# Two of the four weight-quarter sums of each up-projection pair made by accumulating transfers

## The chip, the core and the metric

The kernel runs on one core of one Trainium2 chip. The metric is the device time of one execution in microseconds (us); the runs of the kernel before took 2460.62, 2461.86 and 2464.46 us, so the median is 2461.86 us. Engines are named as in the profile: PE does the matmuls and PEld loads their weights, DVE is the vector engine, ACT the scalar engine, POOL the general one. SP does no arithmetic here and only issues transfers; POOL issues transfers too, from a queue of its own. Every engine works through its own instructions strictly in order, and waits on semaphores of the others.

## The reference, cut to what matters

One layer of a decoder with a model width of 2048, for 512 prompt positions and 8 x 8 sampled ones (576 columns in all). The change touches one product only, `rmsnorm(x, g_ffn) @ w_up`:

```
x  = x + concat(a_out, b_out) @ w_out
up = rmsnorm(x, g_ffn) @ w_up                    # 2048 -> 2 * 5632 = 11264
upc = causal_dwconv(concat(ffn_hist, up), w_dw_f) + b_dw_f    # width 3
x  = x + (silu(upc[..., :5632]) * upc[..., 5632:]) @ w_down
gate = sigmoid(rmsnorm(x, g_ple) @ w_ple_gate)
x  = x + gate * (p @ w_ple_proj)
```

## The kernel before, in words

All tensors are 32-bit floats. The weights stream from memory once, in units of 512 KB: eight tiles of 128x128, side by side, land in one of five buffers of a ring (`raw`), by a transfer that SP issues (`load_unit`, L189). Half a unit (four tiles, 128x512) is a piece. Each piece is split in two by `prepare`: ACT copies it, rounded, to `wh` (L244), and DVE subtracts that from the source to get `wl` (L245); there are four buffers of each. Each weight tile then meets three matmuls: `wh` with the high part of the activations, `wh` with their low part, `wl` with the high part (in the up stage L710, L711 and L712). `weights` calls `prepare` three pieces ahead of the tile in use, and `prepare` calls `add_up` up to two pieces further ahead. These calls set program order; a scheduler then sets each engine's order, and the engines run ahead of one another as far as buffers allow.

The stages, one after another: `mix` (w_in), `out` and `out2` (w_out), `proj` (w_ple_proj), `up` (w_up), four `down` stages, `ple` and a tail. The up stage is 44 pairs. A pair makes the 128 gate channels and the 128 value channels of one hidden tile from 16 x 2 weight tiles, by a scheme with seven products where a plain one has eight: the 16 row tiles are taken as even and odd ones, the two halves of the 576 columns are combined beforehand (`sum_in`, tiles `sx`), and the weights of a pair fall into four quarters of 512 KB, one unit each. Written as a0, a1 (gate channels, even and odd rows) and b0, b1 (value channels), the seven products, in their order, use

- product 5: b0 + b1, in a tile of its own, `sum`
- product 7: b0 + a0, written over b0 in its raw buffer
- product 6: b0 + b1 + a0, written over `sum`
- product 1: a0 as it is
- product 3: b0 + b1 + a1, written over `sum`
- product 4: b1 as it is
- product 2: a1 as it is

A product is 8 weight tiles (2 pieces) x 3 matmuls of 288 columns, so a pair has 14 pieces and 168 matmuls. The four sums are eight DVE additions of 128x512 a pair, all issued at L218: `sum<-raw,raw` for product 5, `raw<-raw,raw` for product 7, `sum<-sum,raw` for products 6 and 3.

The two `sum` tiles of a pair lie in spare places (`SPARE`): two activation tiles `xh`/`xl` for every second pair, and the places of `res14` and `res15` for the others, the first pair among them. Those two are read last by ACT at L580 (`xg`, a step of `sum_in`), shortly before the up stage.

Results of the products are combined at L723 to L733: ACT copies product 1 (`ua`), DVE makes the rest. Product 3's and product 4's results share one PSUM tile, and L729 reads product 3's. The results of 22 of the pairs go to memory by two POOL transfers each (`upd`, L735 and L736); those of the other 22 go through a convolution and a gate, and then to memory by one POOL transfer (`hidd`, L739). In the last pair, 12 hidden tiles are fetched back (`hq`) and split by ACT and DVE (`hh` at L677, `hl` at L678) for the down stages. Around the start of the up stage, 16 POOL transfers (`pjd`, L898) write the results of `proj` from `pa`, which ACT copies out of PSUM (L897), and 16 SP transfers (`xs`) read the new x back for the norm.

Of the kernel before, what the change touches and what calls it, by code (L numbers as in the profile page):

```python
# [11 lines left out]
ALU = mybir.AluOpType  # L12
PSUM = bass.MemoryType.PSUM

P = 128
# [11 lines left out]
NF = DFF // P  # L27
# [33 lines left out]
SUB = 4  # L61


def plan():

    groups = []

    def add(phase, w, outs, ks):  # L70
        groups.append((phase, [(w, m) for m in outs], list(ks)))

    ks = range(KT)

    def gate(i):
        return NA + i

    def val(i):
        return i

    def vee(j):
        return 3 * NA + j

    def you(j):
        return 2 * NA + j

    add("mix", "w_in", [gate(0), val(0), gate(1)], ks)
    add("mix", "w_in", [val(1)], ks)
    for i in range(2, NA):
        add("mix", "w_in", [vee(i - 2)], ks)  # L90
        add("mix", "w_in", [you(i - 2)], ks)
        add("mix", "w_in", [gate(i)], ks)
        add("mix", "w_in", [val(i)], ks)
    add("mix", "w_in", [vee(NB - 2)], ks)
    add("mix", "w_in", [you(NB - 2)], ks)
    add("mix", "w_in", [vee(NB - 1), you(NB - 1)], ks)

    early = [k for k in range(KT) if k not in LATE]
    add("out", "w_out", [0, 1, 2], early)
    for m in range(3, KT):  # L100
        add("out", "w_out", [m], early)
    add("out2", "w_out", [0, 1, 2], LATE)
    for m in range(3, KT):
        add("out2", "w_out", [m], LATE)

    for m in range(KT):
        add("proj", "w_ple_proj", [m], range(DPLE // P))
    for j in range(NF):
        add("up", "w_up", [j, NF + j], ks)

    at = 0
    for c, n in enumerate(CHUNKS):
        js = ORDER[at : at + n]
        at += n
        add(f"down{c}", "w_down", [0, 1, 2], js)
        for m in range(3, KT):
            add(f"down{c}", "w_down", [m], js)

    add("ple", "w_ple_gate", [0, 1, 2], ks)
    for m in range(3, KT):  # L120
        if m not in LAST:
            add("ple", "w_ple_gate", [m], ks)
    for m in LAST:
        add("tail", "w_ple_gate", [m], ks)
    return groups


def weight_order():

    tiles, pieces = [], []
    for phase, outs, ks in plan():
        n = len(tiles)
        if phase == "up":
            (w, a), (_, b) = outs
            for m, odd in ((b, 0), (b, 1), (a, 0), (a, 1)):
                tiles += [(w, k, m) for k in range(odd, KT, 2)]
            pieces += [(n // UNIT, prod, half) for prod in PRODS for half in range(2)]
        else:  # L140
            tiles += [(w, k, m) for k in ks for w, m in outs]
            for s in range(-(-n // SUB), -(-len(tiles) // SUB)):
                pieces.append((s * SUB // UNIT, s % 2))
    assert len(tiles) % UNIT == 0
    return tiles, pieces
# [3 lines left out]
def trunk_kernel(ctx: ExitStack, tc: tile.TileContext, A, O):  # L149
    nc = tc.nc  # L150
    groups = plan()
    order, pieces = weight_order()
    n_w = len(order)

# [4 lines left out]
    def tl(shape, tag, name, bufs=1, dt=F32):  # L159
        return pool.tile(shape, dt, tag=tag, name=name, bufs=bufs)  # L160

    def tmp(name, shape=(P, 2, HT)):
        return tl(list(shape), "t", name, bufs=6)


    raws, parts = {}, {}
# [7 lines left out]
    SPARE = [f"xh{LATE[2]}", f"xl{LATE[2]}", f"res{KT - 2}", f"res{KT - 1}"]  # L174
# [6 lines left out]
    def load_unit(u):  # L181
        if u in raws or u * UNIT >= n_w:
            return
        t = tl([P, UNIT * P], "raw", f"raw{u}", bufs=5)
        if u == 0:
            nc.sync.dma_start(t[:, : SUB * P], A["wstream"][u][:, : SUB * P])
            nc.sync.dma_start(t[:, SUB * P :], A["wstream"][u][:, SUB * P :])
        else:
            nc.sync.dma_start(t, A["wstream"][u])  # L189
        raws[u] = t  # L190

    sums = {}


    NEEDS = {5: 1, 7: 2, 6: 2, 1: 2, 3: 3, 4: 3, 2: 3}

    def quarter(u, n, half):
        return raws[u + n][:, half * SUB * P : (half + 1) * SUB * P]

    def add_up(s):  # L200

        if s in summed_w or s >= len(pieces) or len(pieces[s]) == 2:
            return
        u, prod, half = pieces[s]
        for a in range(NEEDS[prod] + 2):
            load_unit(u + a)
        if prod in (1, 2, 4):
            return
        if prod == 7:
            out = a = quarter(u, 0, half)  # L210
            b = quarter(u, 2, half)
        elif prod == 5:
            out = sums[half] = tl([P, SUB * P], SPARE[2 * (u // 4 % 2) + half], f"sum{u}_{half}")
            a, b = quarter(u, 0, half), quarter(u, 1, half)
        else:
            out = a = sums[half]
            b = quarter(u, 2 if prod == 6 else 3, half)
        nc.vector.tensor_tensor(out=out, in0=a, in1=b, op=ALU.add)  # L218
        summed_w[s] = out

    summed_w = {}

    def prepare(s):
        if s in parts or s >= len(pieces):
            return
        for a in range(s, s + 3):
            add_up(a)
        p = pieces[s]
        if len(p) == 2:
            for a in range(4):  # L230
                load_unit(p[0] + a)
            src = raws[p[0]][:, p[1] * SUB * P : (p[1] + 1) * SUB * P]
        elif s in summed_w:
            src = summed_w[s]
        else:
            src = quarter(p[0], {1: 2, 2: 3, 4: 1}[p[1]], p[2])
        spare = s - (len(pieces) - 4)
        if spare < 0:
            h = tl([P, SUB * P], "wh", f"wh{s}", bufs=4, dt=F32R)
            l = tl([P, SUB * P], "wl", f"wl{s}", bufs=4, dt=F32R)  # L240
        else:
            h = tl([P, SUB * P], HID[32 + 2 * spare], f"wh{s}", dt=F32R)
            l = tl([P, SUB * P], HID[33 + 2 * spare], f"wl{s}", dt=F32R)
        nc.scalar.activation(h, src, AF.Copy)  # L244
        nc.vector.tensor_tensor(out=l, in0=src, in1=h.bitcast(F32), op=ALU.subtract)  # L245
        parts[s] = (h, l)
# [3 lines left out]
    def weights(i=None):  # L250

        n = at["tile"] if i is None else at["tile"] + i
        s = n // SUB
        for a in range(s, s + (4 if s >= 3 else 2)):
            prepare(a)
        if i is None:
            at["tile"] += 1
        h, l = parts[s]
        o = n % SUB * P
        return h[:, o : o + P], l[:, o : o + P]  # L260
# [502 lines left out]
    for gi, (phase, outs, ks) in enumerate(groups):  # L763
# [66 lines left out]
        if gi == 0:  # L830
            prepare(0)
            split_in(0, x0[0], v("g_mix", 0))
            split_in(1, x0[1], v("g_mix", 1))
# [36 lines left out]
        for n, (w, m) in enumerate(outs):  # L870
# [24 lines left out]
            elif w == "w_ple_proj":  # L895
                a = tmp(f"pa{m}")
# [159 lines left out]
```

## Time and profile before

| what | value |
|---|---|
| runs | 2460.62, 2461.86, 2464.46 us |
| profiled execution: time, span | 2461.64 us, 2459.9 us |
| PE busy | 2429.7 us (99%), 18200 matmuls |
| DVE busy | 1838.9 us (75%) |
| ACT busy | 1099.0 us (45%) |
| POOL busy | 92.7 us (4%) |
| traffic | 294.70 MB, mean 120 GB/s |
| up stage | 679.4 to 1677.7 us of the span |

The span is the time between the first and the last event of the profiled execution; 1.7 us of that execution's time lie outside of it. Busy shares are averages over stages with different limits. In rows of the profile a group of instructions is given as line, engine, operation, output and inputs, shapes and count, then busy time, mean time of one, and the idle time before them with what ended it. Rows of a window list give the busy time and count of each engine in a stretch, then the clock that PE was granted (1.00 is full), the share of the 16 transfer engines that was busy, and GB/s.

### The profile page before, as it was taken

The page shows a single profiled execution, that of the slowest core. Times are in us where ns is not written, and L with a number is a line of the kernel's source. Part 1 is how long each engine was busy: PE and PEld are TensorE (multiplying, and loading weights), DVE is VectorE, ACT ScalarE, POOL GpSimd, SP SyncE. Part 2 cuts the span into 40 slices and gives each one's busy share as a digit, 9 for nine tenths or more (in the row PEclk, how much of TensorE's full clock was granted, in tenths as well). Part 3 has the DMA queues.
Part 4 walks back from the last instruction along what each step waited for, and adds up shares of the span by engine and source line. Part 5 has one row for each costly group of instructions (what it writes and reads, how often), then busy time and mean ns, then how long its engine had stood idle before and what let it go on. Part 6 is the DMA issues. An engine that isn't in the chain of part 4 may idle for free. (4 is left out here: it accounts for less than half of the span.)

```text
span 2459.9 us, 45459 instructions
## 1 busy us (share of the span) xinstructions
PE 2429.7 (99%) x18200; PEld 2413.7 (98%) x18200; DVE 1838.9 (75%) x3243; ACT 1099.0 (45%) x2028; POOL 92.7 (4%) x175
## 2 busy tenths in 40 slices
PE   9999999999999999999999999999999999999997
PEld 8999999999999999999999999999999999999997
DVE  7877788885898888888988888887559762254545
ACT  6444445433764454444544444454335441243334
POOL 1000000000200000000000000000000000000000
PEclk9999999999999999999999999999999999999999
DMA  6332222332653334333333333347434442222332
GB/s 237 95 84 84 83 84 84 127 114 89 219 197 119 110 103 126 116 109 117 106 128 114 103 124 111 110 165 269 120 99 150 127 126 86 81 83 86 112 100 96
DMA packets 106196, 294.70 MB, mean 120 GB/s; under 512 B 23568, under 2 KB 27792, under 8 KB 105984
## 3 DMA queue, kind: packets, MB, share of 16 engines
q1 hardware_dynamic: 96096, 259.20, 33.6%
q0 software_dynamic: 9744, 32.60, 3.7%
q8 instruction: 142, 2.33, 0.4%
q14 instruction: 70, 0.57, 0.1%
q10 hardware_dynamic: 144, 0.01, 0.0%
HBM read 255.43 MB, written 36.32 MB: 119 GB/s over the span
## 5 line engine op out<-in xcount | busy, mean ns | idle before, releaser
L244 ACT ACTIVATE wh<-raw 128x512 fp32r<-128x512 f32 x792 | 500.7, 633 | 974.5 <-PE acc L850 669.8
L245 DVE TENSOR_TENSOR wl<-raw,wh 128x512 fp32r<-128x512 f32 x792 | 541.7, 686 | 302.6 <-ACT wh L244 300.9
L710 PE MATMUL acc_up<-sx,wh 128*128 128x288 f32 x2464 | 733.2, 298 | 3.1 <-ACT wh L244 1.5
L712 PE MATMUL acc_up<-sx,wl 128*128 128x288 f32 x2464 | 724.4, 296 | 4.9 <-DVE wl L245 4.8
L711 PE MATMUL acc_up<-sx,wh 128*128 128x288 f32 x2464 | 727.6, 295 | 0.0
L710 PEld LDWEIGHTS acc_up<-sx,wh 128*128 128x128 f32 x2464 | 464.6, 189 | 9.7 <-DVE ua L729 2.6
L712 PEld LDWEIGHTS acc_up<-sx,wl 128*128 128x128 f32 x2464 | 463.4, 189 | 6.4 <-DVE wl L245 6.3
L711 PEld LDWEIGHTS acc_up<-sx,wh 128*128 128x128 f32 x2464 | 464.5, 189 | 0.1
L848 PE MATMUL acc<-xh,wh 128*128 128x288 f32 x1984 | 427.3, 296 | 5.4 <-ACT wh L244 5.3
L850 PE MATMUL acc<-xl,wh 128*128 128x288 f32 x1984 | 424.0, 295 | 0.3 <-DVE xl L286 0.3
L852 PE MATMUL acc<-xh,wl 128*128 128x288 f32 x1984 | 423.5, 294 | 0.0
L848 PEld LDWEIGHTS acc<-xh,wh 128*128 128x128 f32 x1984 | 318.0, 188 | 7.6 <-ACT wh L244 5.3
L850 PEld LDWEIGHTS acc<-xl,wh 128*128 128x128 f32 x1984 | 319.1, 188 | 0.8 <-DVE xl L286 0.6
L852 PEld LDWEIGHTS acc<-xh,wl 128*128 128x128 f32 x1984 | 318.1, 188 | 0.3 <-issue 0.3
L852 PE MATMUL acc<-hh,wl 128*128 128x288 f32 x1408 | 300.9, 295 | 0.0
L848 PE MATMUL acc<-hh,wh 128*128 128x288 f32 x1408 | 300.5, 295 | 0.4 <-DVE x1r L891 0.4
L850 PE MATMUL acc<-hl,wh 128*128 128x288 f32 x1408 | 300.7, 295 | 0.0
L244 ACT ACTIVATE wh<-sum 128x512 fp32r<-128x512 f32 x264 | 166.5, 631 | 224.7 <-PE acc_up L711 212.7
L245 DVE TENSOR_TENSOR wl<-sum,wh 128x512 fp32r<-128x512 f32 x264 | 181.7, 689 | 100.9 <-ACT wh L244 100.8
L848 PEld LDWEIGHTS acc<-hh,wh 128*128 128x128 f32 x1408 | 225.9, 188 | 0.8 <-issue 0.6
L850 PEld LDWEIGHTS acc<-hl,wh 128*128 128x128 f32 x1408 | 225.9, 188 | 0.0
L852 PEld LDWEIGHTS acc<-hh,wl 128*128 128x128 f32 x1408 | 225.9, 188 | 0.0
(191 smaller groups left out, 2143.6 us busy)
## 6 DMA issues: line engine op xcount, KB each, us to landing
raw<-in_wstream SPq DMA_DIRECT2D x395, 512.0 KB
uz<-upd SPq DMA_DIRECT2D x44, 288.0 KB
upd<-ub POOLq DMA_DIRECT2D x22, 288.0 KB, 2.4
upd<-ua POOLq DMA_DIRECT2D x22, 288.0 KB, 2.7
hidd<-hp POOLq DMA_DIRECT2D x22, 288.0 KB, 4.6
hq<-hidd SPq DMA_DIRECT2D x22, 288.0 KB
x<-in_xT SPq DMA_DIRECT2D x16, 288.0 KB
xr<-in_xT SPq DMA_DIRECT2D x16, 288.0 KB
```

The source lines that it names most:

```text
L244: nc.scalar.activation(h, src, AF.Copy)
L245: nc.vector.tensor_tensor(out=l, in0=src, in1=h.bitcast(F32), op=ALU.subtract)
L710: nc.tensor.matmul(dst, wh, bh, start=k == 0, stop=False)
L711: nc.tensor.matmul(dst, wh, bl, start=False, stop=False)
L712: nc.tensor.matmul(dst, wl, bh, start=False, stop=k == KT // 2 - 1)
L848: nc.tensor.matmul(accs[n][:, h, :HT], wh, bh[:, h, :], start=st, stop=False)
L850: nc.tensor.matmul(accs[n][:, h, :HT], wh, bl[:, h, :], start=False, stop=False)
L852: nc.tensor.matmul(accs[n][:, h, :HT], wl, bh[:, h, :], start=False, stop=sp)
```

## The change

The quarters of a pair are streamed in the order b0, a0, a1, b1 where it was b0, b1, a0, a1. The sums of products 5 and 7 are no longer made by DVE. A new function, `transfer_sums`, issues for a pair: on SP, two loads of b0's halves (256 KB each, L209 of the changed kernel) into the two `sum` tiles; on POOL, two transfers of b1's halves (256 KB each, L210) that add to what is in the `sum` tiles; on SP, the load of b0 into a raw buffer, as before; and on POOL one transfer of a0 (512 KB, L212) that adds to this raw buffer. Quarters a0, a1 and b1 are still loaded to raw buffers as well, since later products use them. A pair thus has four DVE additions instead of eight, and its transfers bring 3.5 MB instead of 2 MB from memory, by nine issues instead of four. The additions of products 6 and 3 stay on DVE. `transfer_sums` of a pair is called, at the latest, at product 6 of the pair before. Lines of the changed kernel after this place are 14 higher: `wh` is L258, `pa` L911, `pjd` L912, `hidd` L753, `upd` L749 and L750.

```diff
--- before.py
+++ after.py
@@ -134,7 +134,7 @@
         n = len(tiles)
         if phase == "up":
             (w, a), (_, b) = outs
-            for m, odd in ((b, 0), (b, 1), (a, 0), (a, 1)):
+            for m, odd in ((b, 0), (a, 0), (a, 1), (b, 1)):
                 tiles += [(w, k, m) for k in range(odd, KT, 2)]
             pieces += [(n // UNIT, prod, half) for prod in PRODS for half in range(2)]
         else:
@@ -192,31 +192,45 @@
     sums = {}
 
 
-    NEEDS = {5: 1, 7: 2, 6: 2, 1: 2, 3: 3, 4: 3, 2: 3}
+    NEEDS = {5: 0, 7: 0, 6: 1, 1: 1, 3: 2, 4: 3, 2: 2}
+    first_up = min(p[0] for p in pieces if len(p) == 3)
 
     def quarter(u, n, half):
         return raws[u + n][:, half * SUB * P : (half + 1) * SUB * P]
+
+    def transfer_sums(u):
+
+        if u in begun or u >= first_up + 4 * NF:
+            return
+        begun.add(u)
+        for half in range(2):
+            cols = slice(half * SUB * P, (half + 1) * SUB * P)
+            t = sums[u, half] = tl([P, SUB * P], SPARE[2 * (u // 4 % 2) + half], f"sum{u}_{half}")
+            nc.sync.dma_start(t, A["wstream"][u][:, cols])
+            nc.gpsimd.dma_start(t, A["wstream"][u + 3][:, cols], accum_op=ALU.add)
+        load_unit(u)
+        nc.gpsimd.dma_start(raws[u], A["wstream"][u + 1], accum_op=ALU.add)
+
+    begun = set()
 
     def add_up(s):
 
         if s in summed_w or s >= len(pieces) or len(pieces[s]) == 2:
             return
         u, prod, half = pieces[s]
+        transfer_sums(u)
         for a in range(NEEDS[prod] + 2):
-            load_unit(u + a)
-        if prod in (1, 2, 4):
-            return
-        if prod == 7:
-            out = a = quarter(u, 0, half)
-            b = quarter(u, 2, half)
-        elif prod == 5:
-            out = sums[half] = tl([P, SUB * P], SPARE[2 * (u // 4 % 2) + half], f"sum{u}_{half}")
-            a, b = quarter(u, 0, half), quarter(u, 1, half)
-        else:
-            out = a = sums[half]
-            b = quarter(u, 2 if prod == 6 else 3, half)
-        nc.vector.tensor_tensor(out=out, in0=a, in1=b, op=ALU.add)
-        summed_w[s] = out
+            if (u + a - first_up) % 4:
+                load_unit(u + a)
+            else:
+                transfer_sums(u + a)
+        if prod in (6, 3):
+            t = sums[u, half]
+            nc.vector.tensor_tensor(out=t, in0=t, in1=quarter(u, 1 if prod == 6 else 2, half), op=ALU.add)
+        if prod in (5, 6, 3):
+            summed_w[s] = sums[u, half]
+        if prod == 6 and half == 1:
+            transfer_sums(u + 4)
 
     summed_w = {}
 
@@ -233,7 +247,7 @@
         elif s in summed_w:
             src = summed_w[s]
         else:
-            src = quarter(p[0], {1: 2, 2: 3, 4: 1}[p[1]], p[2])
+            src = quarter(p[0], {7: 0, 1: 1, 2: 2, 4: 3}[p[1]], p[2])
         spare = s - (len(pieces) - 4)
         if spare < 0:
             h = tl([P, SUB * P], "wh", f"wh{s}", bufs=4, dt=F32R)
```

On POOL, at the end of `proj` and the start of the up stage, stood the transfers of `proj` and behind them those of the up stage. Before:

```order
L898 DMA pjd_155<-pa_7832 128x576
L898 DMA pjd_156<-pa_7853 128x576
L898 DMA pjd_157<-pa_7890 128x576
L898 DMA pjd_158<-pa_7911 128x576
L898 DMA pjd_159<-pa_7931 128x576
L736 DMA upd_183<-ub_8099 128x576
L735 DMA upd_182<-ua_8098 128x576
```

Now (`sum_0_7694` and `sum_1_7697` are the first pair's two sums):

```order
L912 DMA pjd_155<-pa_7832 128x576
L912 DMA pjd_156<-pa_7852 128x576
L210 DMA sum_0_7694<-in_wstream 128x512
L912 DMA pjd_157<-pa_7889 128x576
L210 DMA sum_1_7697<-in_wstream 128x512
L912 DMA pjd_158<-pa_7910 128x576
L912 DMA pjd_159<-pa_7930 128x576
L210 DMA sum_0_8236<-in_wstream 128x512
L210 DMA sum_1_8239<-in_wstream 128x512
L212 DMA raw_8242<-in_wstream 128x1024
```

The first pair's accumulating transfers now stand between the last writes of `proj`. Those of the second pair (`sum_0_7941`, `sum_1_7944`) stand further ahead, before `pjd_145`, and the first pair's into its raw buffer stands before `pjd_150`.

On ACT, the first splits of the up stage stood among the last copies of `proj`. Before:

```order
L244 ACTIVATE wh_7796<-sum_0_7696 128x512
L598 ACTIVATE sx_5_7884<-xg_7871 128x576
L244 ACTIVATE wh_7837<-sum_1_7744 128x512
L244 ACTIVATE wh_7895<-raw_7498 128x512
L244 ACTIVATE wh_7942<-raw_7498 128x512
L897 ACTIVATE pa_7890<-acc_0_7856 128x576
L598 ACTIVATE sx_3_7882<-ta_7873 128x576
L897 ACTIVATE pa_7911<-acc_0_7893 128x576
L598 ACTIVATE sx_0_7879<-tb_7874 128x576
L897 ACTIVATE pa_7931<-acc_0_7914 128x576
```

Now:

```order
L612 ACTIVATE sx_5_7883<-xg_7870 128x576
L612 ACTIVATE sx_3_7881<-ta_7872 128x576
L911 ACTIVATE pa_7889<-acc_0_7855 128x576
L911 ACTIVATE pa_7910<-acc_0_7892 128x576
L612 ACTIVATE sx_0_7878<-tb_7873 128x576
L911 ACTIVATE pa_7930<-acc_0_7913 128x576
L258 ACTIVATE wh_7796<-sum_0_7694 128x512
L258 ACTIVATE wh_7836<-sum_1_7697 128x512
L258 ACTIVATE wh_7894<-raw_7498 128x512
```

The first pair's splits have moved behind all of these copies.

In the middle of the up stage, POOL had three writes of results for every two pairs. Before:

```order
L739 DMA hidd_162<-hp_10351 128x576
L736 DMA upd_193<-ub_10266 128x576
L735 DMA upd_192<-ua_10265 128x576
L739 DMA hidd_163<-hp_10888 128x576
```

Now:

```order
L210 DMA sum_0_9867<-in_wstream 128x512
L753 DMA hidd_161<-hp_9823 128x576
L210 DMA sum_1_9870<-in_wstream 128x512
L212 DMA raw_9873<-in_wstream 128x1024
L750 DMA upd_191<-ub_9747 128x576
L749 DMA upd_190<-ua_9746 128x576
L210 DMA sum_0_10121<-in_wstream 128x512
L210 DMA sum_1_10124<-in_wstream 128x512
L212 DMA raw_10127<-in_wstream 128x1024
```

Three accumulating transfers a pair stand among these writes. A write that stands behind one starts only once the accumulating transfer could start.

## The prediction

> **What bounds the kernel now.** I read the page first, then the groups of instructions by line, the list of stretches, and the timelines of the start and the end of the up stage. The page:
>
> ```profile
> PE 2429.7 (99%) x18200; PEld 2413.7 (98%) x18200; DVE 1838.9 (75%) x3243; ACT 1099.0 (45%) x2028; POOL 92.7 (4%) x175
> DVE  7877788885898888888988888887559762254545
> DMA  6332222332653334333333333347434442222332
> ```
>
> PE sets the end. DVE stands at 80 to 90% in the up stage (slices 12 to 27) and the transfer engines at 30 to 40% in most of it, so the change moves work from one engine that is not the bound to another. What it can be worth is in the moments when PE waits in the up stage. Stretches (busy time and count of PE, PEld, DVE, ACT and POOL, then granted clock, share of the transfer engines, GB/s): the whole up stage, and six pieces of it of about a pair's length.
>
> ```profile
> 679.40:1677.70 998.30, 991.74 (x7395) 983.71 (x7396) 863.48 (x1517) 478.85 (x885) 38.76 (x74) 1.00 0.39 124
> 679.40:702.09 22.69, 22.32 (x165) 21.91 (x166) 22.03 (x40) 14.51 (x25) 1.62 (x3) 1.00 0.67 230
> 702.09:724.78 22.69, 22.36 (x168) 22.12 (x168) 22.02 (x38) 12.97 (x22) 1.08 (x2) 1.00 0.64 220
> 838.23:860.92 22.69, 22.69 (x172) 22.56 (x172) 17.59 (x31) 9.17 (x15) 0.54 (x1) 1.00 0.38 119
> 974.37:997.06 22.69, 22.18 (x166) 21.72 (x165) 16.34 (x30) 9.18 (x15) 0.21 (x1) 1.00 0.34 107
> 1473.55:1496.24 22.69, 22.12 (x165) 21.66 (x164) 18.40 (x33) 10.11 (x20) 0.12 (x1) 1.00 0.30 94
> 1587.00:1609.69 22.69, 22.61 (x169) 22.21 (x168) 20.32 (x37) 10.66 (x20) 1.62 (x3) 1.00 0.41 133
> ```
>
> PE idles 998.30 − 991.74 = 6.6 us of the stage. A full stretch holds 172 matmuls, one per 22.69 / 172 = 0.132 us. The others lack 7, 4, 6, 7 and 3. Groups and single moments of PE (busy, mean ns, idle before; in brackets, idle time and what ended it):
>
> ```profile
> L710 PE MATMUL acc_up<-sx,wh 128*128 128x288 f32 x2464 | 733.2, 298 | 3.1 <-ACT wh L244 1.5 <-ACT pa L897 1.5
> L712 PE MATMUL acc_up<-sx,wl 128*128 128x288 f32 x2464 | 724.4, 296 | 4.9 <-DVE wl L245 4.8
> L710 PEld LDWEIGHTS acc_up<-sx,wh 128*128 128x128 f32 x2464 | 464.6, 189 | 9.7 <-DVE ua L729 2.6 <-ACT wh L244 1.9 <-ACT pa L897 1.7
> 679.38 0.40 PE L710 MATMUL acc_up<-sx,wh 128*128 128x288 f32 x1 [1.45 <-ACT pa L897]
> 1664.84 0.40 PE L710 MATMUL acc_up<-sx,wh 128*128 128x288 f32 x1 [1.14 <-ACT wh L244]
> 1668.91 0.61 PE L712 MATMUL acc_up<-sx,wl 128*128 128x288 f32 x1 [3.54 <-DVE wl L245]
> ```
>
> So 1.14 + 3.54 = 4.7 of the 6.6 us lie in the last pair, 1.45 us lies just ahead of the stage, and only 1.9 us is idle in the 43 pairs between. Whatever DVE is freed of, this is nearly all that can come back.
>
> **What is removed.** Two of four sums, four additions a pair:
>
> ```profile
> L218 DVE TENSOR_TENSOR sum<-raw,raw 128x512 f32<-128x512 f32 x88 | 60.2, 686 | 6.8 <-DMA raw<-in_wstream 3.7 <-ACT xg L580 2.5
> L218 DVE TENSOR_TENSOR raw<-raw,raw 128x512 f32<-128x512 f32 x88 | 58.5, 685 | 15.3 <-DMA raw<-in_wstream 15.3
> ```
>
> That is 118.7 us of DVE, 2.7 us a pair of some 22.5. Nearly all of it lies beside matmuls. What comes back is the short stalls: by idle time 1.9 us; by missing matmuls (7 + 4 + 6 + 7 + 3) × 0.132 = 3.6 us, since a late matmul is shown as a long one. Pair 13 shows what such a stall is:
>
> ```profile
> 989.00:990.50 1.50, 0.99 (x7) 0.53 (x5) 1.50 (x5) 0.54 (x1) 0.00 (x0) 1.00 0.71 199
> ```
>
> DVE was busy all the time and PE got 7 matmuls instead of 11. With half of the additions gone such bursts shrink, so I take the middle, **−2.7 us**; bounds 0 (the bursts come from other work) and −3.6. DVE L729 holds product 4's first matmul in every pair, 2.6 us of weight-load idle in all. That operation must wait for product 3's last matmul, and a shorter queue only spares what stands ahead of it: I take a quarter, **−0.6**, bounds −2.6 and +2.6 (the new order puts something else ahead of it).
>
> The last pair gains nothing from DVE's relief. Its wait is behind ACT and DVE, which split 12 fetched tiles there:
>
> ```profile
> 1665.00:1670.00 5.00, 1.46 (x6) 1.15 (x7) 4.82 (x10) 1.56 (x4) 0.00 (x0) 0.81 0.47 151
> 1670.00:1675.00 5.00, 5.00 (x23) 5.00 (x23) 0.69 (x1) 0.63 (x1) 0.00 (x0) 0.51 0.97 256
> ```
>
> DVE is full at 4.82 of 5.00, but the last additions lie before these rows, and the orders of ACT and DVE there are what they were: 0, bounds ±2 by the fetches (`hq`), which share the transfer engines with fewer or more loads.
>
> **What is added in a steady pair.** 1.5 MB a pair from memory in about 22.7 us is 66 GB/s more on 119 (the row of 838.23); in proportion the transfer engines' share goes from 0.38 to about 0.6. An accumulating transfer is in no row. The nearest are POOL's writes (KB, median us from issue to landing):
>
> ```profile
> upd<-ub POOLq DMA_DIRECT2D x22, 288.0 KB, 2.4
> hidd<-hp POOLq DMA_DIRECT2D x22, 288.0 KB, 4.6
> x1d<-x POOLq DMA_DIRECT2D x16, 288.0 KB, 3.5
> ```
>
> SP's loads have no time there, so I give them the same. So 2.4 to 4.6 us for 256 KB; I take 3.5, and for 512 KB 4.6, with 2.4 (the least of 288 KB) and 9.2 (twice the largest) as bounds. Do they land before their reader? Pair 8, from the timelines:
>
> ```profile
> 826.84 0.68 DVE L245 TENSOR_TENSOR wl<-sum,wh 128x512 fp32r<-128x512 f32 x1
> 834.14 0.54 POOL L739 DMA_DIRECT2D hidd<-hp  x1 [38.66 <-DVE hp L662]
> 839.25 0.69 DVE L245 TENSOR_TENSOR wl<-raw,wh 128x512 fp32r<-128x512 f32 x1
> 857.50 0.69 DVE L245 TENSOR_TENSOR wl<-sum,wh 128x512 fp32r<-128x512 f32 x1 [1.52 <-ACT wh L244]
> 860.53 0.69 DVE L245 TENSOR_TENSOR wl<-raw,wh 128x512 fp32r<-128x512 f32 x1
> ```
>
> The `sum` tile is free at 827.5, loaded by about 830; POOL's second accumulation stands behind `hidd` (834.14 + 0.54) and ends about 838.2. The first reader is at 857: 19 us of slack. The raw buffer is free at 839.9; a load of 4.6 and an accumulation of 4.6 end at 849.1, ACT's reader is about 859.8: 10.7 us of slack. So a steady pair costs **0**. The cover is gone when load and accumulation of 512 KB together take over some 20 us. The writes `upd` stand behind the accumulation into the raw buffer and are only later by some us; nothing reads them before the end of the stage.
>
> **What moves at the start.** There no pair's lead exists. The first pair's `sum` tiles are the last places that ACT's `xg` reads:
>
> ```profile
> 673.80 1.43 ACT L580 ACTIVATE xg<-x,vec 128x576 f32<-128x576 f32 x2
> 674.60 0.69 DVE L218 TENSOR_TENSOR sum<-raw,raw 128x512 f32<-128x512 f32 x1 [2.51 <-ACT xg L580]
> 675.47 0.62 ACT L244 ACTIVATE wh<-sum 128x512 fp32r<-128x512 f32 x1
> ```
>
> Before, DVE needs 0.69 us from the release at 674.6 on. Now SP's load (2.4) and POOL's accumulation (2.4 to 4.6) follow one another: 679.4 to 681.6. ACT's `wh` takes 0.6: the first up matmul is at 680.0 to 682.2, where it stood at 679.38, so +0.7 to +2.9; I take +1.8. In order, ACT now has these splits behind all copies of `proj`, so the copies, which set the 1.45 us, no longer wait for splits: no loss by that. DVE's `wl` comes after `wh`, +0.5.
>
> Ahead of it, the second pair's two tiles are free early (they belong to `out2`), so their loads and accumulations, and the first pair's raw b0 with its 512 KB, fall in `proj`, whose chain already runs through transfers:
>
> ```profile
> 662.50:665.00 2.50, 2.50 (x21) 2.50 (x20) 1.57 (x4) 2.50 (x5) 1.07 (x2) 1.00 1.19 333
> 667.52 0.65 ACT L897 ACTIVATE pa<-acc 128x576 f32<-128x576 f32 x1 [2.30 <-DMA pjd<-pa]
> 668.22 0.53 PE L848 MATMUL acc<-ph,wh 128*128 128x288 f32 x2 [1.29 <-ACT pa L897]
> ```
>
> At 662.5 the transfer engines are full (1.19) and PE then waits 1.29 us for `pa`, which waits for a `pjd` write to leave its buffer. With 1.5 MB more (at 333 GB/s, 4.5 us of transfer), and `pjd` writes queued on POOL behind accumulations that wait for their own loads, this grows; I take +1.0, bounds 0 and +4.5. The start: 1.8 + 0.5 + 1.0 = **+3.3**, bounds +0.7 and +2.9 + 0.5 + 4.5 = +7.9.
>
> **Sum.** +3.3 − 2.7 − 0.6 + 0 + 0 = 0.0. The profiled execution took 2461.64 us (span 2459.9), 0.2 below the median of the runs, 2461.86. Forecast: **2461.6 us**, the same. From the bounds: −5.5 to +10.5, which would need all at once; for this case alone 2457 to 2467.
>
> **Rivals.**
>
> A. *The start halves the clock.* After 3.54 us without matmuls the end of the stage shows granted clocks of 0.81 and 0.51; in the 5 us at 0.51 there were 23 matmuls instead of 38, so 2 to 3 us lost. Before, PE waits 1.45 us at 679.38; my +1.8 makes 3.3, and +2.9 makes 4.4. If the accumulation takes the long bound, and `proj` loses its 4.5: +7.9 + 2.9 − 3.3 = +7.5, **2469 us**. It decides once the gap passes some 3.5 us. For it: no lead at the start, and ACT and POOL wait in order there. Against: 2.4 us is as likely a transfer time as 4.6.
>
> The Trainium skill ("TensorE: Matmul & The Clock Gate", Part 1: The HAM clock gate) has PE fall to half clock after an idle window of about 3.4 us, and back after about as long busy. The trace agrees (3.54 us, then 0.51), and by that rule a gap from 677.9 to 682.2 would pay it.
>
> The Trainium skill ("DMA: Bandwidth & Descriptors", Anatomy of one DMA — SWDGE (gpsimd) path) has a POOL transfer take 2.0 us plus its bytes at 436 GB/s: an estimate of 2.6 us for 256 KB. By it the start's +1.8 would be about +0.9 and the sum −0.9.
>
> B. *The accumulations are slow in every pair.* If adding to a tile runs at a fraction of a copy's pace, or the loads slow each other at the higher share, the slack of 10.7 us goes: each us over it costs 44 pairs × 1 us. At 1 us over, 2461.6 + 44 = **2506 us**; it decides from about 15 us for an accumulation of 512 KB (4.6 + 10.7). For it: the path is in no row; three accumulations a pair share POOL's order. Against: 15 us is three times the longest POOL write.
>
> C. *DVE's relief reaches further.* If the start costs the least (+0.7), all 3.6 us of stalls and 2.6 at L729 go, and `hq` fetches at the end come 2 us earlier: +0.7 − 3.6 − 2.6 − 2 = −7.5, **2454 us**; with the 3.54 us gap at the end shortened, clock loss too. For it: DVE at 22.0 of 22.7 us in the first pairs. Against: only 1.9 us of idle outside the last pair.
>
> D. The change doesn't do what it says: the additions stay or the transfers run on one after another. The order shows it does; no chance kept.
>
> **Chances.** Forecast 0.56; A 0.18; B 0.11; C 0.15. The range must leave out no more than 2 in 10: from C's upper part, 2455, to past A, 2473. A measurement of this kernel tells 0.2% (4.9 us) from no change: below 2456.9 is faster, above 2466.8 slower. C gives faster, 0.15; A and B give slower, 0.29; the rest is 0.56.
>
> **What would show it.** Right: L218 has 176 instructions fewer, DVE about 119 us less in the up stage, PE's idle time there 3 to 4 us less outside of the last pair, no PE wait that is ended by a `wh<-sum` or `wh<-raw` behind an accumulation in steady pairs, a share of transfer engines near 0.6, and a PE gap before the first up matmul of 2.5 to 4.5 us. Wrong: a granted clock under 1.00 right after 680 (A), 44 equal gaps ended by accumulating transfers (B), a last pair without its 3.54 us gap (C).

## The result and the profile after

The changed kernel takes 2476.86 us (median of five runs, 2474.0 to 2481.07) against 2463.63 us for the kernel before on the same chip (median of five as well, 2460.62 to 2464.46). The ratio is 1.0057, with a 95% interval of 1.0042 to 1.0072: slower by 0.57%. The forecast was 2461.6 us, no change; 2476.86 lies above the top of its range, 2473. The profiled execution is the one of 2476.86 us, with a span of 2474.8 us.

From the page of the changed kernel: engine rows and the two queues that carry data (packets, MB, share of the 16 engines' span).

```profile
PE 2432.0 (98%) x18200; PEld 2417.3 (98%) x18200; DVE 1751.8 (71%) x3067; ACT 1098.8 (44%) x2028; POOL 207.9 (8%) x307
q1 hardware_dynamic: 108768, 282.27, 36.1%
q0 software_dynamic: 28752, 78.74, 14.7%
```

DVE has 176 instructions fewer, as forecast, but is only 87 us less busy than before, not 119: the page counts time in which two instructions of an engine overlap once, and added up one by one DVE's instructions take 116 us less. PE has the same 18200 matmuls, and its idle time has grown from 30.2 us (2459.9 − 2429.7) to 42.8 us.

Where did the time go? The starts of the 18200 matmuls of both profiled executions, put side by side, tell it. Lateness of the changed kernel against the one before:

| place | late by, us |
|---|---|
| `proj`, before the first gap | −0.4 |
| last matmul of `proj` | 7.9 |
| first matmul of the up stage | 13.1 |
| middle of the first pair | 14.5 |
| end of the third pair | 18.9 |
| end of the up stage | 14.8 |
| end of the kernel | 14.9 |

So about 19 us are lost between the end of `out2` and the third pair, some 4.0 us come back over the next 41 pairs (0.7 of them in the last), and the rest of the kernel is as it was. In the steady stage the change does what was forecast. The same 600 us, first of the kernel before:

```profile
900.00:1500.00 600.00, 598.92 (x4486) 594.61 (x4486) 519.28 (x919) 283.34 (x534) 22.43 (x44) 1.00 0.36 114
```

and of the changed kernel:

```profile
900.00:1500.00 600.00, 600.00 (x4505) 596.69 (x4505) 466.46 (x810) 282.39 (x530) 93.55 (x125) 1.00 0.71 185
```

PE has no idle time left at all and does 19 matmuls more, 2.5 us' worth, while the transfer engines' share doubles from 0.36 to 0.71. The start is another matter. The waits of PE there, and the two of the last pair, from the timeline (in brackets idle time and what ended it):

```profile
668.02 0.85 PE L862 MATMUL acc<-ph,wh 128*128 128x288 f32 x2 [7.87 <-ACT pa L911]
692.52 0.61 PE L724 MATMUL acc_up<-sx,wh 128*128 128x288 f32 x1 [6.67 <-ACT wh L258]
735.06 0.37 PE L724 MATMUL acc_up<-sx,wh 128*128 128x288 f32 x1 [1.97 <-DVE uu L738]
1680.34 0.40 PE L724 MATMUL acc_up<-sx,wh 128*128 128x288 f32 x1 [1.13 <-ACT wh L258]
1684.41 0.61 PE L726 MATMUL acc_up<-sx,wl 128*128 128x288 f32 x1 [3.55 <-DVE wl L259]
```

Before, the first two were 1.29 and 1.45 us, and the third was not there. The last pair's waits are unchanged (1.14 and 3.54 before). After each of the three the granted clock is low for some us:

```profile
665.00:670.00 5.00, 1.98 (x8) 1.98 (x9) 0.73 (x2) 2.64 (x5) 1.09 (x2) 0.50 0.46 184
690.00:695.00 5.00, 2.48 (x9) 2.26 (x10) 1.78 (x3) 1.70 (x4) 0.00 (x0) 0.50 1.01 295
735.00:740.00 5.00, 4.44 (x20) 4.24 (x21) 4.49 (x9) 1.98 (x4) 2.22 (x3) 0.66 0.90 206
```

The clock (the eighth column) was halved for 6.8, 6.8 and 3.4 us; PE was at work for 3.7, 3.1 and 3.4 us of these, which adds about 1.5 to 2 us to the lateness each time. How the first two gaps came about is read from the chain of waits between 650 and 700, in order of time (start, duration, what; the rows in between, nearly all of PE at work, are left out). The first gap:

```profile
650.77 6.76 DMA sum<-in_wstream
657.60 0.50 issue
658.12 1.38 POOL sum L210 x2
659.53 7.70 DMA pjd<-pa
667.32 0.66 ACT pa L911
```

and the second:

```profile
681.78 0.67 ACT xg L594
682.47 3.40 DMA sum<-in_wstream
685.94 0.50 issue
686.45 5.36 DMA sum<-in_wstream
691.84 0.64 ACT wh L258
```

In the first, SP loads the second pair's `sum` tiles (6.76 us), POOL waits for that with its accumulations, a write of `proj` (`pjd`) stands behind them and lands 7.70 us after its issue, and only then does ACT get a free buffer to empty PSUM, the memory that PE writes to. In the second, from the release of the first pair's tiles at 682.47 on, load and accumulation take 3.40 + 0.5 + 5.36 us one after the other. The third is ACT waiting for reads of x: the group of ACT's squares (busy, mean ns, idle before, what ended most of it), first before, then after:

```profile
L298 ACT ACTIVATE sq<-xs 128x576 f32<-128x576 f32 x15 | 10.1, 676 | 3.7 <-DMA xs<-x1d 3.7
```

```profile
L312 ACT ACTIVATE sq<-xs 128x576 f32<-128x576 f32 x15 | 10.2, 679 | 16.6 <-DMA xs<-x1d 16.6
732.47 0.69 ACT L312 ACTIVATE sq<-xs 128x576 f32<-128x576 f32 x1 [2.94 <-DMA xs<-x1d]
733.06 0.61 ACT L258 ACTIVATE wh<-raw 128x512 fp32r<-128x512 f32 x1
733.58 0.39 ACT L737 ACTIVATE ua<-acc_up 128x288 f32<-128x288 f32 x1
```

In ACT's order a split of weights and the copy of product 1 stand behind the square of 732.47. DVE's `uu` needs that copy, and PE's wait of 1.97 us is put down to `uu`.

### The profile page after: what moved, and what is told of

Read it like the earlier page. It is cut to its first block, busy times and chain, and to the rows that moved or that the text cites. A ratio compares the mean times of both kernels' runs of the same rounds, so it can differ in the third digit from the quotient of the medians.

```text
span 2474.8 us, 45750 instructions
## 1 busy us (share of the span) xinstructions
PE 2432.0 (98%) x18200; PEld 2417.3 (98%) x18200; DVE 1751.8 (71%) x3067; ACT 1098.8 (44%) x2028; POOL 207.9 (8%) x307
## 3 DMA queue, kind: packets, MB, share of 16 engines
q1 hardware_dynamic: 108768, 282.27, 36.1%
q0 software_dynamic: 28752, 78.74, 14.7%
## 4 chain that ended last, share of the span: by engine, by line
PE 95%; DMA 2%; DVE 1%; ACT 1%; issue 0%; SPq 0%; POOL 0%; DVEq 0%; ACTq 0%; POOLq 0%
PE acc L862 18%; PE acc L864 18%; PE acc L866 18%; PE acc_up L724 13%; PE acc_up L726 13%; PE acc_up L725 13%; DMA xs<-x1d 1%; DMA sum<-in_wstream 1%; DMA pjd<-pa 0%; PE vps L521 0%; DVE wl L259 0%; PE mps L559 0%; DVE y L972 0%; PE acc L936 0%; PE acc L937 0%
## 5 line engine op out<-in xcount | busy, mean ns | idle before, releaser
L258 ACT ACTIVATE wh<-raw 128x512 fp32r<-128x512 f32 x792 | 500.0, 632 | 971.3 <-PE acc L864 671.4
L258 ACT ACTIVATE wh<-sum 128x512 fp32r<-128x512 f32 x264 | 166.4, 630 | 221.2 <-PE acc_up L725 213.2
```

## Experiments

The expectations give a gap from the start of the last matmul ahead of it, which comes to 0.3 us more than the idle time in the rows (8.17, 6.97 and 2.27 us for 7.87, 6.67 and 1.97). Three questions: what makes each gap, whether the accumulations cost where they have their lead (are begun a pair ahead of their use), and what DVE's relief is worth.

**First three pairs the old way.** A pair below the limit keeps the old order of quarters and DVE's additions; the others are as in the change.

```diff
-for m, odd in ((b, 0), (a, 0), (a, 1), (b, 1)):
+for m, odd in (((b, 0), (b, 1), (a, 0), (a, 1)) if a < 3 else ((b, 0), (a, 0), (a, 1), (b, 1))):
...
+    def by_dve(u):
+        return u < first_up + 4 * 3
...
+        if by_dve(u):
...
+            if prod == 6 and half == 1:
+                transfer_sums(u + 4)
+            return
```

> Edit: the first three pairs have the old order of quarters and their sums made by DVE; the other 41 have theirs made by accumulating transfers as in the change. Theory (all that was lost lies at the start of the up stage: PE gaps of 8.17 us at 659.85, 6.97 us at 685.55 and 2.27 us at 732.79 of the changed kernel, with a halved clock after each; the steady pairs gain): the three gaps go, the gap before the first up matmul is 1.75 us again, the short stalls of three later pairs (0.9 + 0.9 + 0.4 us by the pair lengths 23.29, 23.35 and 22.79 against 22.41) and 0.7 us in the last pair come back: 2 to 4 us faster than the kernel before, about 2460 against 2463.6. Rival (the slow accumulating transfers cost wherever they begin): new gaps in the fourth and fifth pair, 2466 or more.

Measured: 2461.44 us (2458.01 to 2463.66) against 2460.78, ratio 1.0 (0.9991 to 1.0008). The whole loss is gone, so it lay in the first three pairs and ahead of them. But the gain of 2 to 4 us was not there either. In the profiled execution it is 4.2 us late at the end of the third pair, and 3.8 us of that come back over the rest of the stage. The second pair is longer than before (23.84 against 22.9 us): the first accumulating transfers, those of the fourth pair, begin in it at 720, among the reads of x. The first pair is longer too (24.83 against 23.2 us), before any of them has begun; what makes that was not found.

**Only the first pair the old way** (`a < 1`).

> Edit: only the first pair is made the old way; the second pair's accumulating transfers still fall into the stage before. Theory (three separate causes: writes of proj behind the second pair's accumulations; the first pair's load and accumulation one after the other; SP's order held back by a full ring): the second cause goes, so the gap before the first up matmul falls from 6.97 to about 1.75 us, while a gap of 5 to 9 us stays near 660: 2467 to 2472. Rival (the first pair's own transfers, its 512 KB accumulation among them, make both gaps): both gaps go, 2464 or less.

Measured: 2469.83 us, ratio 1.004 (1.0025 to 1.0056). PE's two longest waits there (a third in `proj` is 0.81 us):

```profile
664.71 0.54 PE L888 MATMUL acc<-ph,wh 128*128 128x288 f32 x2 [3.11 <-ACT pa L937]
684.04 0.40 PE L750 MATMUL acc_up<-sx,wh 128*128 128x288 f32 x1 [2.20 <-ACT pa L937]
```

The wait before the up stage is down from 6.67 to 2.20 us and is again one for `pa`: the second cause was the first pair's own transfers. The time fell as the theory said. The gap near 660 is smaller than the 5 to 9 us it expected, so the first pair's accumulation into its raw buffer had a part in it. That one lies in `out2`, from 644.18 to 651.33 in the changed kernel; the one at 671.36, which stands before `pjd_150` between the writes of `proj`, is the second pair's and not the first's (it is still there when only the first pair goes the old way, and gone when only the second does).

**Only the second pair the old way** (`a == 1`), the complement.

> Edit: only the second pair is made the old way; the first pair's sums are transfers. Theory (the engines are full in the stage before because of the second pair's sums, 3.4 us of the gap near 660, and of the first pair's 512 KB accumulation, the rest): the gap near 660 falls from 8.17 to 2.5 to 5.5 us, the gap of about 7 us before the first up matmul stays at 4.5 us or more, time 2467 to 2473. Rival (either of the two accumulations alone is enough to make the whole gap): gap near 660 stays at 7 us or more.

Measured: 2472.43 us, ratio 1.0046 (1.0032 to 1.006).

```profile
661.57 0.54 PE L888 MATMUL acc<-ph,wh 128*128 128x288 f32 x2 [0.80 <-ACT pa L937]
669.41 0.53 PE L888 MATMUL acc<-ph,wh 128*128 128x288 f32 x2 [1.22 <-ACT pa L937]
685.37 0.61 PE L750 MATMUL acc_up<-sx,wh 128*128 128x288 f32 x1 [6.26 <-ACT wh L284]
```

The start's wait stays at 6.26 us, and near 660 and 669 there are 2.0 us, little more than the 1.29 of before and less than the 2.5 to 5.5 expected. Waits in `proj` are 1.3 us with neither pair's transfers, 2.0 with the first's alone, 3.9 with the second's alone, 7.9 with both: more than their sum, in one trace of each. In both runs the first three pairs still lose time: 6.3 us with the first pair the old way and 8.4 with the second, by the starts of the matmuls, where the change loses 5.7 (the halved clock included).

**Is it POOL's order or the transfer engines' time?** The writes of `proj` are issued by ACT on its own queue:

```diff
-                nc.gpsimd.dma_start(proj_d[m], a)
+                nc.scalar.dma_start(proj_d[m], a)
```

> Edit: the changed kernel, with the 16 writes of proj's results issued by ACT on its own queue instead of POOL's. Theory (order: on POOL and in its queue these writes stand behind accumulating transfers): the 8.17 us gap near 660 falls below 2.5 us, the later 6.97 us gap stays at 4 us or more, and the time falls by 6 to 10 us to 2467 to 2471. Rival (the transfer engines are simply full there): the gap near 660 stays over 5 us and the time within 3 us of the changed kernel's 2476.9.

Measured: 2477.82 us, ratio 1.0069 (1.0055 to 1.0083), no better than the change itself.

```profile
662.86 0.53 PE L862 MATMUL acc<-ph,wh 128*128 128x288 f32 x2 [1.46 <-ACT pa L911]
665.01 0.53 PE L862 MATMUL acc<-ph,wh 128*128 128x288 f32 x2 [0.30 <-ACT pa L911]
668.27 0.53 PE L862 MATMUL acc<-ph,wh 128*128 128x288 f32 x2 [1.43 <-ACT pa L911]
675.80 0.85 PE L862 MATMUL acc<-ph,wh 128*128 128x288 f32 x2 [4.11 <-ACT pa L911]
669.36 0.33 ACTq L912 DMA_DIRECT2D pjd<-pa  x1
675.09 1.38 ACT L911 ACTIVATE pa<-acc 128x576 f32<-128x576 f32 x2 [3.91 <-DMA pjd<-pa]
```

The gap is spread out, and its sum is 7.30 us against 7.87. So the theory of order falls: a write that stands behind nothing of POOL's is as late. The last one issued before ACT's wait of 3.91 us went out at 669.36, so the write waited for took at least 5.7 us; before the change the median was 2.8. The edit isn't clean, since a write now stands in ACT's order (one whose data were ready at 662.80 was issued at 664.38), and the wait before the up stage grew to 7.52 us. The Trainium skill ("DMA: Bandwidth & Descriptors", Issuing engines are not separate DMA queues) says that transfers begun by different engines run on the same 16 transfer engines and interleave; this run agrees, with 7.30 us of waits left on a queue of its own.

**The same transfers without adding.** POOL's three transfers of a pair overwrite their tile. That leaves out the adding: product 5 gets b1 alone, product 7 a0 alone, and products 6 and 3 lack b0. (Product 3 adds a1 to the tile of product 6, so in the kernels before and after the change it holds all four quarters.) Orders and bytes are unchanged.

```diff
-            nc.gpsimd.dma_start(t, A["wstream"][u + 3][:, cols], accum_op=ALU.add)
+            nc.gpsimd.dma_start(t, A["wstream"][u + 3][:, cols])
...
-        nc.gpsimd.dma_start(raws[u], A["wstream"][u + 1], accum_op=ALU.add)
+        nc.gpsimd.dma_start(raws[u], A["wstream"][u + 1])
```

> Edit: the changed kernel, with the three POOL transfers of each pair overwriting their tile instead of adding to it, so that products 5, 7, 6 and 3 use one quarter in place of a sum (work left out); orders, bytes from memory and waits are the same. Theory (the gaps come from waits in order, and the adding itself has a part in them because an accumulating transfer holds the engines about twice as long per byte: 46 MB took 11% of the span against 36% for 282 MB of loads): the gaps near 660 and 686 shrink but stay, 3 us or more each, time 2467 to 2474, and POOL's transfers take about 4 us instead of 6.2. Rival 1 (adding costs nothing): within 2 us of 2476.9. Rival 2 (adding is the whole cost): no gap over 2.5 us, 2462 or less.

Measured: 2467.74 us, ratio 1.0029 (1.0019 to 1.0039). PE's longest waits, the queue's row of the page, and transfers with their time to landing:

```profile
663.56 0.54 PE L862 MATMUL acc<-ph,wh 128*128 128x288 f32 x2 [2.01 <-ACT pa L911]
686.74 0.61 PE L724 MATMUL acc_up<-sx,wh 128*128 128x288 f32 x1 [6.00 <-ACT wh L258]
q0 software_dynamic: 23120, 78.74, 9.7%
raw<-in_wstream POOLq DMA_DIRECT2D x44, 512.0 KB, 4.8
sum<-in_wstream POOLq DMA_DIRECT2D x88, 256.0 KB, 4.2
pjd<-pa POOLq DMA_DIRECT2D x16, 288.0 KB, 3.7
```

and the last three of the changed kernel:

```profile
raw<-in_wstream POOLq DMA_DIRECT2D x44, 512.0 KB, 6.4
sum<-in_wstream POOLq DMA_DIRECT2D x88, 256.0 KB, 6.2
pjd<-pa POOLq DMA_DIRECT2D x16, 288.0 KB, 5.6
```

Adding is what fills the engines. POOL's queue holds them for 9.7% of the span without it and 14.7% with it; the same row of the kernel before has 32.60 MB and 3.7%. The new 46 MB thus cost 6.0% as copies and 11.0% as additions: 1.8 times as much for the same bytes. The loads of the other queue took 36.1% and 35.9%, so it is not waiting that is counted. The packets differ as well (28752 and 23120), since the copies of 256 KB went in packets of 4 KB instead of 2 KB; but POOL's packets of 4 KB alone took 0.38 us each on average with adding and 0.20 us without. Without adding, the gap in `proj` shrinks from 7.87 to 2.01 us (and 0.41 and 0.17 us at two later places), with the order on POOL as it was. PE's waits in `proj` are thus 1.3 us before the change, 2.6 with POOL's order alone, 7.3 with adding alone, and 7.9 with both. And ACT's wait for reads of x falls from 16.6 to 9.0 us in all. The gap before the up stage is hardly touched, 6.00 us: it is two transfers in a row. The time fits the theory; its "3 us or more each" holds for the second gap only.

**The places of the sums exchanged**, so that the first pair's `sum` tiles are the ones that come free early.

```diff
-            t = sums[u, half] = tl([P, SUB * P], SPARE[2 * (u // 4 % 2) + half], f"sum{u}_{half}")
+            t = sums[u, half] = tl([P, SUB * P], SPARE[2 * ((u // 4 + 1) % 2) + half], f"sum{u}_{half}")
```

> Edit: the changed kernel with the two places of the sums exchanged: the first pair's sums go where the stage before frees its place first (at its start), the second pair's to the places of res14 and res15. Theory (the gap before the first up matmul is load and accumulation one after the other behind the release of res14 and res15): the gap of 6.97 us falls below 2.5 us, while the gap near 660 stays at 6 us or more since the same bytes lie there, time 2468 to 2472. Rival (full transfer engines make the start late whatever the place): the gap stays over 4.5 us, time 2475 or more.

Measured: 2469.71 us, ratio 1.0035 (1.0023 to 1.0047), as the theory said. The waits of PE above half a us from 658 to 706:

```profile
665.86 0.85 PE L862 MATMUL acc<-ph,wh 128*128 128x288 f32 x2 [4.18 <-ACT pa L911]
697.71 0.40 PE L724 MATMUL acc_up<-sx,wh 128*128 128x288 f32 x1 [0.60 <-ACT wh L258]
704.09 0.37 PE L724 MATMUL acc_up<-sx,wh 128*128 128x288 f32 x1 [2.32 <-DVE uu L738]
```

The first up matmul, at 684.24, follows the last of `proj` without a gap. Missing lead made that wait. Not all of it was gained: the gap in `proj` became 4.18 us, less than the 6 expected, but the first pair now takes 28.3 us where the change takes 24.0, with the wait of 2.32 us at 704.09 and ACT waiting 18.9 us in all for reads of x. That the time came out as forecast is so in part luck.

**The reads of x issued by ACT**, to see if SP's order holds them back.

```diff
-        nc.sync.dma_start(x, x1_d[m])
+        nc.scalar.dma_start(x, x1_d[m])
```

> Edit: the changed kernel with the 16 reads of x in the first pairs issued by ACT instead of SP. Theory (the gap of 2.27 us in the second pair is ACT waiting to square an x whose read stands on SP behind a weight load that waits for a ring buffer): that gap falls below 1 us, the two gaps before stay, time 2471 to 2475. Rival (full transfer engines delay the read itself, on any queue): the gap stays at 1.5 us or more, time 2476 or more.

Measured: 2479.67 us, ratio 1.0072 (1.0057 to 1.0087).

```profile
L312 ACT ACTIVATE sq<-xs 128x576 f32<-128x576 f32 x15 | 10.3, 685 | 26.8 <-DMA xs<-x1d 26.8
734.15 0.33 ACTq L757 DMA_DIRECT2D xs<-x1d  x1
737.01 0.69 ACT L312 ACTIVATE sq<-xs 128x576 f32<-128x576 f32 x1 [0.84 <-DMA xs<-x1d]
```

The waits grew. But the edit brought one of its own: ACT issues a read only when it comes to the square of the one before (734.15), and 2.9 us later squares it. So this run doesn't tell SP's order from full engines. For the read behind the third gap the trace of the changed kernel does:

```profile
728.28 0.33 SPq L189 DMA_DIRECT2D raw<-in_wstream  x1
728.66 0.42 SPq L757 DMA_DIRECT2D xs<-x1d  x1
```

The weight load of 728.28 had waited 7.2 us on SP for a buffer of the ring. The read behind it, issued at 728.66, was squared 3.8 us later, at 732.47; the reads that ACT waited for before the change took 3.9 to 4.7 us. So this read was late by SP's order and not by a slow transfer. But the buffer itself came free late, by a `wl` whose `wh` stood on ACT behind an earlier wait for a read; and the four reads that ACT waited for ahead of this one took 5.3 to 8.9 us, which fits full engines, as does the run without adding. How much of the loss belongs to each stays open.

**First five pairs the old way**, so that the accumulations begin when the reads of x are over; run twice.

> Edit: the first five pairs the old way, so that the first accumulating transfers begin in the fifth pair, when the reads of x (16 transfers, squared by ACT) are over. Theory (with three pairs the old way, the transfers of the fourth pair still fell among these reads and cost about 1.5 us in the second pair, which hid the gain of 3 to 4 us later): 2457 to 2460 against some 2461.2 before, ratio 0.9983 to 0.9995. Rival (the gain in the trace is a matter of which execution was profiled): ratio 0.9996 to 1.0005, the same as with three.

> Edit: the first five pairs the old way once more, to narrow the interval (0.9984 to 1.0002 the first time). Theory (the trace's gain of some 3.5 us is there in most executions): ratio 0.9985 to 0.9995. Rival (no gain): 0.9996 to 1.0004.

Measured: 2459.28 us (2457.34 to 2461.35) against 2460.46, ratio 0.9993 (0.9984 to 1.0002), and 2459.42 us (2458.05 to 2463.32) against 2462.01, ratio 0.9992 (0.9983 to 1.0001). The medians are 1.2 and 2.6 us lower, and each interval just takes in no change. In the trace the gain is plain. The same 600 us as above, in the first of the two runs:

```profile
900.00:1500.00 600.00, 600.00 (x4503) 596.55 (x4502) 469.66 (x817) 284.49 (x536) 91.48 (x123) 1.00 0.70 185
```

PE is never idle there, the start is as before (waits of 1.50 and 1.41 us), and the profiled executions end 3.4 and 3.3 us earlier than the one of before; both were about 1 us faster than the median of their runs. A gain is likely but not shown. It is the best version found, and at most a thousandth or so better than the kernel before.

**DVE's relief alone.** In the kernel before, the four additions of products 5 and 7 are left out, with no transfer in their place; products 5 and 7 use b0 alone, 6 and 3 lack b1. Product 6 then makes the first sum, so the order of DVE's work and the use of the buffers change as well.

```diff
-        if prod in (1, 2, 4):
+        if prod in (1, 2, 4, 5, 7):
             return
-        if prod == 7:
...
+        if prod == 6:
+            out = sums[half] = tl([P, SUB * P], SPARE[2 * (u // 4 % 2) + half], f"sum{u}_{half}")
+            a, b = quarter(u, 0, half), quarter(u, 2, half)
```

> Edit: the kernel before, with the four additions a pair of products 5 and 7 left out (product 5 and 7 use b0 alone, product 6 b0 + a0, product 3 b0 + a0 + a1; work left out); no transfer is added. This is what DVE's relief alone can bring. Theory (the short stalls of the pairs are DVE's, the rest of DVE's work lies beside matmuls): the stalls in pairs 13, 35 and 40 go, with about 0.7 us of the last pair and up to 1.5 us in the first three pairs: 3 to 5 us, ratio 0.9980 to 0.9990. Rival (those stalls are other work's, and the freed 2.7 us a pair bring nothing): ratio 0.9993 or more.

Measured: 2464.46 us against 2462.01, ratio 1.0012 (1.0003 to 1.0021): not faster, a little slower.

```profile
900.00:1500.00 600.00, 598.42 (x4479) 593.41 (x4478) 463.03 (x811) 281.90 (x532) 21.99 (x43) 1.00 0.35 114
1236.50:1238.50 2.00, 1.65 (x12) 1.42 (x11) 2.00 (x6) 0.63 (x1) 0.00 (x0) 1.00 0.87 248
L709 PE MATMUL acc_up<-sx,wl 128*128 128x288 f32 x2464 | 726.2, 296 | 7.9 <-DVE wl L242 6.5
```

DVE has as much work in these 600 us (463 us) as in the changed kernel (466.46), yet PE does 26 matmuls fewer. The long stalls of the 14th and 36th pair went, but that of the 41st grew (23.98 us, 22.79 before), and nearly every second pair got a new one of 0.2 us, a `wl` that comes late while DVE is full (2.00 of 2.00 at 1236.5). So less work on DVE doesn't by itself remove the stalls. That they hang on where the rest stands in DVE's order is likely; what makes them was not tried.

## Why the prediction was wrong, point by point

- **What bounds the kernel.** Right: PE, with 1.9 us of idle time between the first and the last pair, so that little could come back. About 4.0 us did, 0.7 of them in the last pair.
- **The stalls of DVE, −2.7.** About right: the 14th, 36th and 41st pair, 23.29, 23.35 and 22.79 us before by the starts of their matmuls, take 22.39 now. That is −2.3 us, within the bounds of 0 and −3.6; the rest of the 3.6 lay in the first pairs, which lost. The reason given, fewer additions and so shorter bursts, was only half of it: with the same additions left out and nothing in their place the stalls moved instead of going.
- **Product 4's wait, −0.6.** About right in size: a steady pair is 22.39 us, where it was mostly 22.41 or 22.42, about −1.0 over the pairs. Of the weight loads' waits for DVE's `ua` (L729) the trace before lists 14 above 0.15 us, where the prediction has one in every pair; the trace after lists none. That the gain comes from them alone was not shown.
- **The last pair, 0.** Right: waits of 1.13 and 3.55 us stay; it is 0.7 us shorter, 29.4 against 30.1, within the ±2.
- **A steady pair, 0.** Right, with numbers that were too low. An accumulation takes 6.2 to 6.4 us to land, not 3.5 and 4.6, and the share of the transfer engines is 0.71, not 0.6, because adding costs 1.8 times a copy (without adding the same 600 us have 0.57). The slack of 10.7 and 19 us covers that, and rival B did not come. The prediction's other estimate for 256 KB on POOL, 2.6 us, was further off: 4.2 us without adding, 6.2 with.
- **The start, +3.3.** This step failed. Of it:
  - The term for `proj`, +1.0 with bounds of 0 and +4.5, measured +8.3 with its clock. It took the added bytes at the pace of the stage's loads (333 GB/s) and gave an accumulation a copy's time. The runs put most of the difference on adding: 7.87 us of wait with it, 2.6 without. The queue on POOL, which the step named as well, was not the point: 7.3 us were left without it. Of the bytes that it put into `proj`, the first pair's 512 KB came earlier, in `out2`, and the second pair's 512 KB of a0, added at 671.36, were not counted. And no clock was reckoned for this gap, which halved it.
  - The term for the first matmul, +1.8 and +0.5, measured +5.2, and 1.4 more for the clock after it. The mechanism was right, load and accumulation in a row behind the release of the tiles: the exchange of places takes the wait away. The sizes were 3.40 + 0.5 + 5.36 us in place of 2.4 and 2.4 to 4.6.
  - A term was missing: +4.4 from the middle of the first pair to the end of the third. The reads of x for the norm lie there, ACT's splits stand behind its squares of them, and its wait for them went from 3.7 to 16.6 us. Without adding, it is 0.6 us over the same matmuls. The prediction named these reads nowhere.
- **Rival A** (the start's gap halves the clock) is what happened, with the chance of 0.18 and a price of +7.5 us; the trace shows about +15, since two more gaps did the same. The halved clock itself makes about 5 of the 19 us lost at the start; the waits are the rest. Its first number, the gap from 3.5 us on, held in the first two: after 7.87 and 6.67 us the clock was 0.50. After the third, 1.97 us in this row and another 0.5 us right after it, the granted clock was 0.66 too, while a wait of 3.11 us at 664.71, with only the first pair the old way, left it at 1.00. So no single length of one wait decides in these runs. The Trainium skill ("TensorE: Matmul & The Clock Gate", Part 1: The HAM clock gate) names an idle window of about 3.4 us for the drop; the first two gaps agree with it, the third, two waits of 1.97 and 0.50 us with two matmuls between, came to less.

The sum by the measured terms, from −0.4 on: −0.4 + 8.3 (`proj`, its clock included) + 5.2 + 1.4 (first matmul and clock) + 4.4 (first pairs) − 4.0 = +14.9, as between the two spans.

## What to carry to other kernels

Work that is moved from an engine with time to spare to the transfer engines has to be paid in each stage's own share of them, not in the mean: here a share of 0.71 cost nothing in 41 pairs, and 1.5 to 2 MB in and just ahead of a short stage that already reached a share of 0.98 cost 8 us. A transfer that is begun ahead has no lead in the first round, so the first rounds are best left as they were; the trial of that gave back the whole loss. And a bound for an operation that no row shows must be wider than the nearest rows, when the operation does more than these do.

## What the runs showed of the hardware that was not expected

- An accumulating transfer into SBUF holds the transfer engines 1.8 times as long as a copy of the same bytes from memory (11.0% against 6.0% of the span for 46 MB), and lengthens the transfers beside it: writes of 288 KB landed in 5.6 us, 3.7 without adding, 2.8 before the change.
- The waits that it makes in a full stage did not add up: 2.0 and 3.9 us of waits with one of two sets of transfers, 7.9 with both.
- The granted clock of PE was halved for 3.4, 6.8 or 10.2 us at a time, up to the last matmuls of all twelve traces. With only the first pair the old way, waits of 1.44 and 0.49 us close together were followed by it, and a wait of 3.11 us was not.
- PE's matmuls run undisturbed beside transfer engines that are 71% busy: 4505 matmuls in 600 us, without idle time.
- Taking 2.7 us out of DVE's 19.4 us a pair (519.28 us in 600) left the kernel a little slower (1.0012). The order of what is left changed with it; that this is the cause was not shown.
